# A decoder block with 32 routed experts: slots by row count, and expert weights addressed from registers

## The chip, the cores and the metric

The kernel runs on one core of a Trainium2 chip. The metric is device time in microseconds (us) of one execution, the median of the runs shown. Engines: PE (TensorE, matmul), DVE (VectorE), ACT (ScalarE), POOL (GpSimd), SP (SyncE, which here only issues DMAs); 16 DMA engines move data between the device's memory and the core.

## The reference

One layer of a decoder block: a token mixing half (two attention groups and an output projection) and a channel mixing half of routed experts. The change lies in the second half, which is

```python
def moe_ffn(h, w_router, b_router, w_mlp1, b_mlp1, w_mlp2, b_mlp2):   # 512 rows of 1024, 32 experts, top 4
    logits = xf @ w_router + b_router
    top_val, top_idx = lax.top_k(logits, TOP_K)
    gates = jax.nn.softmax(top_val, axis=-1)
    ...
    def expert_block(args):                          # the rows of one expert, e its number
        hid = xb @ w_mlp1[e] + b_mlp1[e]             # 1024 -> 2048
        glu = jnp.minimum(hid[..., ::2], SWIGLU_LIMIT)
        lin = jnp.clip(hid[..., 1::2], -SWIGLU_LIMIT, SWIGLU_LIMIT)
        act = glu * jax.nn.sigmoid(SWIGLU_ALPHA * glu) * (lin + 1.0)
        return act @ w_mlp2[e] + b_mlp2[e]           # 1024 -> 1024
    ...
    out = jax.ops.segment_sum(y * slot_gate, slot_tok)

x = x + gt2 * rms_norm(moe_ffn(h2, ...), g_post_ffn)
```

All tensors are float32. Each of the 512 rows goes to 4 of 32 experts, so an expert has 64 rows on average. The weights of one expert are 8 MB and 4 MB.

## The kernel before

**Order of the work.** The kernel is written as a list of operations. A planner (class `Plan`) orders them per engine: it simulates the engines with a cost for each operation, takes at each step the operation that can start first (ties by its place in the text plus a shift for its section), and gives out buffers as it goes. Each engine then runs its instructions strictly in that order, SP and POOL with their DMA issues too. All instructions are emitted from one place, so the profile shows nearly all of them on line 568. Tiles `u` are large buffers, `w` middle, `tiny` small ones, `bank` is a PSUM bank.

**Before the experts.** Attention and the output projection; then for each of four tiles of 128 rows: the norm (`wo_post`), router logits, top 4, gates and each row's place within its expert (`route`, lines 1426 to 1464). Places are in `posm16`, gates in `gate` and, split in three bfloat16 parts, in `aux`. `cnt` (1541) counts the rows of each expert, for a loop at the end (2065) that handles rows over 96 in extra blocks; its count is read into a register on every engine (2063). `b1` (1560) loads all biases into `b1r`, split in a high and a low part.

**One expert.** All 32 experts are handled alike, in the order of their number, with 96 slots each. `list_of` turns places into a list of row numbers for four experts at a time; `gather` (1619) fetches 96 rows of h2 by an indirect DMA on POOL, two experts ahead; `x_transposes` turns them. `bias_mm` starts three PSUM banks with the bias. `mm1` takes one load of weights (128 rows of `w_mlp1`, 1 MB) and multiplies; `swiglu`, `act_transposes`, then `mm2` with one load of `w_mlp2` (256 rows, 1 MB). An expert is 8 + 4 loads. `y_out` scales by the gate and `scatter` (1637) adds the 96 rows into an accumulator in the device's memory by an indirect DMA on POOL.

**Column tiles.** PE is used as four column tiles of 32 columns that work at the same time. With 96 slots there are three groups of 32 slots and four quarters of the output, 12 pieces, laid over three banks:

```python
def item(b, g):
    return (b, g) if g < 3 else (3, b)
```

**Weight loads.** `w_load` (1511) issues the loads on SP in a fixed sequence `seq` (1504): the first layer of expert e, then the second layer of expert e - 1. Up to ten loads (`DEPTH`) are ahead: load n waits for PE to have finished load n - 10 (1531). Addresses are constants.

**The end.** The last expert is not scattered. Its second layer comes in four loads of another shape; `split_last` splits each into a high and a low part on ACT, DVE and POOL, and `mm_last` multiplies the parts. `combine` (1810), in three column ranges, adds the last expert to the sums by a selecting matmul, adds the gated biases of the second layer, takes the norm and the residual and writes the output. `load_sums` (1801) reads the accumulator back, four tiles of 512 KB.

Of the kernel before, what the change touches and what calls it, by code (L numbers as in the profile page):

```python
# [26 lines left out]
E = 32  # L27
# [14 lines left out]
SLOTS = 96  # L42
EXTRA = 4
# [7 lines left out]
END_DVE = tuple((h, i) for h in (1, 2) for i in range(4))  # L51
SEL_RAW = (1, 2)
# [79 lines left out]
class Off:  # L132


    def __init__(self, view):
        self.view = view

# [137 lines left out]
class Plan:  # L275
# [107 lines left out]

    def after(self, o, *xs):
        for x in xs:
            o.deps[x.idx] = x
        return o
# [182 lines left out]
    @staticmethod  # L570
    def real(a):
        if isinstance(a, View):
            return a.real()
        if isinstance(a, Off):
            return bass.IndirectOffsetOnAxis(ap=a.view.real(), axis=0)
        return a


def build(tc, I, out, dbg=None):
# [752 lines left out]
    for t, b, g in ((gt1g, 0, 0), (gs2b, 1, 0), (sh2b, 0, 2)):  # L1332
# [22 lines left out]
                    op=ALU.add)  # L1355
    selb = const([P, 16, 12], F32, "selb")
    for b in range(3):
        V.tensor_copy(selb[:, :, 4 * b:4 * b + 3], selr[:, :, b:b + 1].to_broadcast([P, 16, 3]))
        V.tensor_copy(selb[:, :, 4 * b + 3:4 * b + 4], selr[:, :, 3:4])
# [6 lines left out]
    posm16 = const([P, NT, E], F16, "posm16")  # L1366
    cnt = const([P, E], F32, "cnt")
    aux = const([P, NT, E, 5], BF16, "aux")
# [57 lines left out]
    def route(i, r2):  # L1426
        with pl.sect(f"route{i}"):
# [31 lines left out]
            V.tensor_copy(aux[:, i, :, 2], gate[:, i, :])  # L1459
            g1 = small([P, E])  # L1460
            V.tensor_tensor(g1, gate[:, i, :], aux[:, i, :, 2], op=ALU.subtract)
            V.tensor_copy(aux[:, i, :, 3], g1)
            V.tensor_tensor(g1, g1, aux[:, i, :, 3], op=ALU.subtract)
            V.tensor_copy(aux[:, i, :, 4], g1)
# [45 lines left out]

    def w_load(n):
        e, s, j = seq[n]
        t = big((P, 2, D))
        if s and e == ne - 1:


            r, h = divmod(j, 2)
            src = w2_d[e * D + 512 * r:e * D + 512 * (r + 1), 512 * h:512 * (h + 1)].rearrange("(k p) n -> p k n", p=P)
            if j < 3:
                o = SP.dma_start(t.rearrange("p k (a n) -> p (k a) n", n=512), src)  # L1520
            else:
                for q in range(2):
                    o = SP.dma_start(t[:, q].rearrange("p (k n) -> p k n", n=256), src[:, :, 256 * q:256 * q + 256])
        elif s:

            o = SP.dma_start(t, w2_d[e * D + 256 * j:e * D + 256 * (j + 1), :].rearrange("(p k) n -> p k n", k=2))
        else:
            o = SP.dma_start(t.rearrange("p k n -> p (k n)"), w1[e * D + P * j:e * D + P * (j + 1), :])
# [11 lines left out]

    pl.gate = marks[6]
    with pl.sect("cnt"):

        pc = PS()
        with pl.group():
            for i in range(NT):
                T.matmul(pc[:, 0:E], lhsT=onesb, rhs=mkb[:, i, :], start=(i == 0), stop=(i == NT - 1))
        V.tensor_copy(cnt, pc[:, 0:E])
        NB = EXTRA * E
        fl = const([P, NB], F32, "fl")  # L1550
        for b in range(EXTRA):
            V.tensor_scalar(fl[:, b * E:(b + 1) * E], cnt, float(SLOTS + P * b), None, op0=ALU.is_gt)
        zero = small([P, NB])
        V.memset(zero, 0.0)
        incl = const([P, NB], F32, "incl")
        V.tensor_tensor_scan(incl, fl, zero, 0.0, ALU.add, ALU.add)
        nx_i = const([P, 1], I32, "nx_i")
        V.tensor_copy(nx_i, incl[:, NB - 1:NB])

    with pl.sect("b1"):  # L1560

        b1r = pl.buf((P, 2 * D), F32R, keep=True)
        for name, n in (("b_mlp1", 512), ("b_mlp2", 256)):
            b = w2((P, n))
            bH, bL = w2((P, n), F32R), w2((P, n), F32R)
            SP.dma_start(b, I[name].rearrange("l e (r n) -> (l e r) n", n=n))
            if n == 512:
                V.tensor_scalar(b[:, 1::2], b[:, 1::2], 1.0, None, op0=ALU.add)  # L1570
            A.copy(bH, b)
            V.tensor_tensor(bL, b, bH.bitcast(F32), op=ALU.subtract)
            for k, part_ in enumerate((bH, bL)):
                if n == 512:
                    for h in range(2):
                        SP.dma_start(b1r[64 * k:64 * k + 64, 512 * h:512 * h + 512].bitcast(F32),
                                     part_[64 * h:64 * h + 64, :].bitcast(F32))
                else:
                    SP.dma_start(b1r[64 + 32 * k:96 + 32 * k, D:2 * D].bitcast(F32), part_.bitcast(F32))

    pl.gate = None
# [4 lines left out]
    def one_hot(e, dt):  # L1586
        oh = w2((P, NT, SLOTS), dt)
        V.tensor_tensor(oh, slot16[:, 0:SLOTS].unsqueeze(1).to_broadcast([P, NT, SLOTS]),
                        posm16[:, :, e:e + 1].to_broadcast([P, NT, SLOTS]), op=ALU.is_equal)
        return oh  # L1590

    def list_of(es):
# [21 lines left out]
        for t in range(3):  # L1614
            V.tensor_copy(gg[96:128, 1 + t, :n], gg[32 * t:32 * t + 32, 0, :n])
        for a, e in enumerate(es):
            lists[e] = si[:, a:a + 1], gg[:, :, a:a + 1], gi[:, a:a + 1]
# [24 lines left out]
    def item(b, g):  # L1642
        return (b, g) if g < 3 else (3, b)
# [274 lines left out]
    def real(v):  # L1918
        return v.real()
# [171 lines left out]
```

## Time and profile before

| | |
|---|---|
| median of 3 runs | 1467.78 us (1466.84 to 1472.5) |
| the profiled execution's own time | 1467.23 us |
| its span, first to last instruction | 1465.5 us |
| mean granted clock of PE | 0.977 |
| busy: PE, DVE, ACT, POOL | 1405.5, 481.9, 283.3, 136.3 us |
| moved by DMA | 485.13 MB, 331 GB/s over the span |
| first weight step of the experts, and last scatter | 322.87 us, 1399.3 us |

How to read it: times are from one profiled execution. A group is a line, an engine, an operation and its tiles, with its count, its busy time, the mean of one in ns, and the idle time of the engine ahead of it with what ended that. PEld is the loading of PE's stationary side. DMA share is the mean busy share of the 16 engines. A busy PE includes modelled ends of pipelined matmuls.

### The profile page before, as it was taken

What the parts mean: (1) busy time and instruction counts of PE and PEld (TensorE: products, weight loads), DVE (VectorE), ACT (ScalarE), POOL (GpSimd) and SP (SyncE); (2) the same over time, 40 slices, a digit from 0 to 9 for tenths busy, and PEclk for the clock granted to TensorE, in tenths of its full rate; (3) what the DMA queues carried; (4) which work ended last, traced back from release to release, by engine and by line L of the source; (5) the groups of instructions that cost most, each with busy time, mean ns of one, the idle gap of its engine ahead of it and who ended that gap; (6) DMA issues with size and microseconds to landing.
All of it is one profiled execution on the core that took longest, in us unless ns stands there. A gap on an engine that the chain in (4) does not pass through costs nothing.

```text
span 1465.5 us, 33208 instructions
## 1 busy us (share of the span) xinstructions
PE 1405.5 (96%) x14622; PEld 681.9 (47%) x14622; DVE 481.9 (33%) x1310; ACT 283.3 (19%) x654; POOL 136.3 (9%) x182
## 2 busy tenths in 40 slices
PE   4999999989999999999999999999999999999985
PEld 2766568773444444444444444444444444434433
DVE  5689996771112211221211121122111211111134
ACT  4553596311010100010000000010100100011022
POOL 3000000400000000001000000000000001000023
PEclk8999999969999999999999999999999999999996
DMA  9928425349999999999999999999999999999951
GB/s 322 272 95 324 167 84 191 127 168 353 390 391 396 378 367 394 394 390 395 391 383 391 389 391 377 398 398 393 392 396 394 393 385 399 391 370 393 370 191 59
DMA packets 99297, 485.13 MB, mean 331 GB/s; under 512 B 14831, under 2 KB 33682, under 8 KB 48462
## 3 DMA queue, kind: packets, MB, share of 16 engines
q1 hardware_dynamic: 92206, 458.59, 80.6%
q0 software_dynamic: 6944, 24.38, 6.9%
q8 instruction: 116, 1.90, 0.5%
q14 instruction: 31, 0.25, 0.0%
HBM read 460.31 MB, written 20.07 MB: 328 GB/s over the span
## 4 chain that ended last, share of the span: by engine, by line
PE 88%; DVE 5%; DMA 3%; SPq 2%; issue 1%; ACT 1%; POOL 0%; DVEq 0%; POOLq 0%; ACTq 0%
PE bank L568 88%; DVE u L568 2%; SPq L568 2%; DVE w L568 2%; DMA u<-in_w_ada_dram 1%; DVE tiny L568 1%; DMA u<-qpart 1%; DMA u<-in_w_kv_b_dram 1%; ACT w L568 0%; DMA u<-h2d,tiny 0%; ACT u L568 0%; DVE aux L568 0%; DVE x L568 0%; DVE u L1967 0%; POOL tiny L568 0%
## 5 line engine op out<-in xcount | busy, mean ns | idle before, releaser
L568 PE MATMUL bank<-u,u 128*32 128x512 f32 (+2 forms) x12840 | 1176.8, 482 | 1.9 <-DVE w L568 0.9
L568 PEld LDWEIGHTS bank<-u,u 128*32 128x32 f32 (+1 forms) x12840 | 509.6, 115 | 600.5 <-issue 440.4
L568 DVE TENSOR_SCALAR u<-bank 128x256 f32<-128x256 f32 x96 | 38.7, 421 | 511.3 <-ACT u L568 281.1
L568 ACT ACTIVATE u<-bank 128x256 f32<-128x256 f32 x96 | 36.5, 383 | 550.0 <-PE bank L568 541.5
L568 DVE TENSOR_SCALAR u<-bank,tiny 96x256 f32<-96x256 f32 (+1 forms) x124 | 60.5, 488 | 239.0 <-PE bank L568 237.4
L568 POOL DMA_INDIRECT acc<-u,tiny x31 | 46.0, 1483 | 955.2 <-DVE w L568 663.6
L568 ACT COPY u<-bank 128x384 f32<-128x384 f32 (+3 forms) x115 | 50.0, 440 | 229.4 <-PE bank L568 207.3
L568 PE MATMUL bank<-ident,u 96*128 96x96 f32 (+1 forms) x472 | 66.5, 281 | 15.3 <-DVE u L568 13.6
L568 PEld LDWEIGHTS bank<-ident,u 96*128 96x128 f32 (+1 forms) x472 | 53.1, 172 | 57.6 <-issue 34.7
L568 DVE COPY u<-bank 128x64 f32<-128x64 f32 (+3 forms) x140 | 42.5, 342 | 111.6 <-PE bank L568 65.8
L568 PE MATMUL bank<-w,u 128*64 128x128 f32 (+4 forms) x472 | 55.8, 309 | 10.8 <-DMA u<-qpart 4.1
L568 ACT ACTIVATE u<-bank,tiny 96x512 f32<-96x512 f32 x31 | 21.2, 683 | 221.5 <-PE bank L568 221.5
L568 PEld LDWEIGHTS bank<-w,u 128*64 128x64 f32 (+1 forms) x472 | 45.7, 179 | 22.8 <-issue 11.8
L568 DVE TENSOR_TENSOR u<-u,u 128x1024 fp32r<-128x1024 f32 (+6 forms) x53 | 44.2, 853 | 6.7 <-ACT u L568 6.4
L568 DVE SCALAR_TENSOR_TENSOR u<-u,u 128x256 f32<-128x256 f32 (+1 forms) x99 | 43.5, 468 | 1.2
L568 ACT CAST u<-u 128x1024 fp32r<-128x1024 f32 (+4 forms) x48 | 36.2, 799 | 30.6 <-PE bank L568 20.7
L568 POOL DMA_INDIRECT u<-h2d,tiny x31 | 31.2, 1007 | 58.7 <-DVE tiny L568 20.3
L568 PE MATMUL bank<-u,w 128*128 128x512 f32 x104 | 34.9, 442 | 0.3 <-DVE w L568 0.2
L568 PE MATMUL bank<-u,condT 128*32 128x512 f32 x192 | 26.1, 639 | 8.5 <-DMA u<-in_w_ada_dram 7.2
L568 ACT COPY w<-bank 64x512 f32<-64x512 f32 (+5 forms) x67 | 29.9, 474 | 22.1 <-PE bank L568 18.0
L568 PE MATMUL bank<-ident,w 128*128 128x128 f32 (+2 forms) x192 | 29.6, 279 | 3.8 <-DVE w L568 2.0
L568 PE MATMUL bank<-w,w 128*128 128x512 f32 (+5 forms) x88 | 32.1, 468 | 0.9 <-DVE w L568 0.6
(155 smaller groups left out, 594.8 us busy)
## 6 DMA issues: line engine op xcount, KB each, us to landing
u<-in_w_mlp_dram SPq DMA_DIRECT2D x383, 1024.0 KB
u<-in_w_ada_dram SPq DMA_DIRECT2D x16, 1024.0 KB
u<-in_w_ada_dram SPq DMA_DIRECT2D x16, 512.0 KB
u<-in_w_o_dram SPq DMA_DIRECT2D x8, 512.0 KB
u<-in_w_in_dram SPq DMA_DIRECT2D x7, 512.0 KB
acc<-u SPq DMA_DIRECT2D x5, 512.0 KB
x<-in_x_dram SPq DMA_DIRECT2D x4, 512.0 KB
u<-in_w_in_dram SPq DMA_DIRECT2D x2, 1024.0 KB
```

The lines of the kernel that those rows point to most:

```text
L568: f(*[self.real(a) for a in args], **{k: self.real(a) for k, a in kw.items()})
```

## The change

**Positions.** The experts are handled in 32 positions instead of by number. Positions 0 to 3 hold experts 0 to 3, with 96 slots. The other 28 experts are sorted by their number of rows on the chip; the 16 largest go to positions of 96 slots, the 12 others to positions of 64 (`POS_RANK`: three of every eight positions, and the last two).

**Arranging.** A function `arrange`, called when expert 1 is set up, counts the rows, ranks the 28 experts by comparing all pairs (DVE on 28 x 28), writes the expert number of each position to `perm`, and permutes places, gates and counts (`posp16`, `gatep`, `cntp`). SP then reads the 28 expert numbers into registers, and the weight loads from position 4 on take their address from them. The biases of the first layer are gathered in position order by an indirect DMA; those of the first four come in directly, ahead.

**64 slots.** Two PSUM banks instead of three, `item` lays 2 x 4 pieces over them; gather, transposes, SwiGLU and scatter shrink alike. **The end:** the last expert has 64 slots and uses `mm2` like the others; `split_last` and `mm_last` are gone; `combine` works on two halves of 512 columns, with the bias matmuls of six of eight parts ahead of the last weights. **Extra blocks** use `perm` and the room of each position.

```diff
+FULL = 16
+POS_RANK = []
+_big, _small = list(range(FULL)), list(range(FULL, E - NS))
+for _n in range(E - NS):
+    POS_RANK.append((_small if _n >= E - NS - 2 or _n % 8 in (1, 4, 6) else _big).pop(0))
+ROOM = [96] * NS + [96 if _r < FULL else 64 for _r in POS_RANK]
...
+    def value(self, view, lo, hi):
+        v = Value(self.nc.sync, lo, hi)
+        c = ("SP", v, "value_load", (view,), {}, [], [view], (60.0, 0))
+        return v, self.add([c], None)
...
     def w_load(n):
         e, s, j = seq[n]
         t = big((P, 2, D))
-        if s and e == ne - 1:
...
+        def rows_of(src, r, m):
+            if e < NS:
+                return src[e * D + r:e * D + r + m, :]
+            return src[bass.ds(which[e][0].value * D + r, m), :]
+        if s:
+            o = SP.dma_start(t, Lazy(lambda: rows_of(w2_d, 256 * j, 256).rearrange("(p k) n -> p k n", k=2)))
         else:
-            o = SP.dma_start(t.rearrange("p k n -> p (k n)"), w1[e * D + P * j:e * D + P * (j + 1), :])
+            o = SP.dma_start(t.rearrange("p k n -> p (k n)"), Lazy(lambda: rows_of(w1, P * j, P)))
+        if e >= NS:
+            pl.after(o, which[e][1])
...
+    def arrange():
+        m = E - NS
...
+        with pl.sect("cnt"):
+            pc = PS()
+            with pl.group():
+                for i in range(NT):
+                    T.matmul(pc[:, 0:E], lhsT=onesb, rhs=mkb[:, i, :], start=(i == 0), stop=(i == NT - 1))
+            V.tensor_copy(cnt, pc[:, 0:E])
+            key, rank = small([P, m]), small([P, m])
+            V.scalar_tensor_tensor(key, cnt[:, es], float(E), tie[:, es], op0=ALU.mult, op1=ALU.add)
+            rows_by_cols(along(key), across(key), ALU.is_gt, rank)
+            put = rows_by_cols(along(rank), across(rpos[:, es]), ALU.is_equal)
+            V.tensor_copy(perm[:, 0:NS], ecol[:, 0:NS])
+            rows_by_cols(put, along(ecol[:, es]), ALU.mult, perm[:, es])
+            perm_i = const([1, E], I32, "perm_i")
+            V.tensor_copy(perm_i, perm[0:1, :])
+            for p in range(NS, ne):
+                which[p] = pl.value(perm_i[0:1, p:p + 1], NS, E - 1)
             for i in range(NT):
+                places = small([P, m])
+                rows_by_cols(put, along(posm16[:, i, es]), ALU.mult, places)
+                V.tensor_copy(posp16[:, i, es], places)
+                rows_by_cols(put, along(gate[:, i, es]), ALU.mult, gatep[:, i, es])
+                gate_parts(i, es)
+        with pl.sect("b1"):
...
+            G.indirect_dma_start(out=b, out_offset=None, in_=b1_d, in_offset=Off(frm), bounds_check=P - 1, oob_is_err=True)
...
+            halves_of(b, 512, lambda k: [(64 * k, 512 * h, slice(64 * h, 64 * h + 64)) for h in range(2)])
...
     def gather(e):
-        xg = big((SLOTS, D))
+        xg = big((ROOM[e], D))
...
-    def item(b, g):
+    def item(m, b, g):
+        if m == 64:
+            return 2 * b + g // 2, g % 2
         return (b, g) if g < 3 else (3, b)
...
-            for b in range(3):
+            for b in range(len(hid)):
                 for g in range(4):
-                    n, t = item(b, g)
+                    n, t = item(m, b, g)
...
+            if e == 1:
+                arrange()
...
-        act = act_transposes(fa, True)
-        y = [PS()[0:SLOTS, 0:n] for n in (512, 256, 256)]
+        act = act_transposes(fa)
+        y = [PS()]
+        open_ = {(i, h): bias_of(i, h) for i in range(3) for h in range(2)}
         for j in range(4):
-            w = split_last()
-            r = j // 2
-            mm_last(y[1:] if j % 2 else y[:1], lambda c: (act[:, 4 * r + c, :], act[:, 8 + 4 * r + c, :]), w, j < 2, j == 3)
-            for h in {2: (0,), 3: (1, 2)}.get(j, ()):
-                combine(h)
+            mm2(y, act, j)
+        combine(y[0], open_)
```

The five steps of `route` that split the gates of 32 experts become `gate_parts` on four columns, with two copies of four columns ahead (places and gates of experts 0 to 3); the constants that `arrange` needs are filled on GpSimd with 44 small instructions ahead of the experts.

More of the change, by code (lines that the diff above doesn't have):

```diff
@@ L136, in __init__, with value_load @@
         self.view = view
+class Lazy:
+    def __init__(self, make):
+        self.make = make
+class Value:
+    def __init__(self, engine, lo, hi):
+        self.engine, self.lo, self.hi, self.value = engine, lo, hi, None
+    def value_load(self, ap):
+        self.value = self.engine.value_load(ap, min_val=self.lo, max_val=self.hi)
 class Buf:
@@ L1458, in route, with gate_parts @@
             V.tensor_scalar(gate[:, i, :], ex, sg, None, op0=ALU.mult)
[L1459 to L1464, printed above, removed]
+            for to, frm in ((posp16, posm16), (gatep, gate)):
+                V.tensor_copy(to[:, i, 0:NS], frm[:, i, 0:NS])
+            gate_parts(i, slice(0, NS))
+    def gate_parts(i, es):
+        a = aux[:, i, es]
+        g1 = small([P, es.stop - es.start])
+        V.tensor_copy(a[:, :, 2], gatep[:, i, es])
+        V.tensor_tensor(g1, gatep[:, i, es], a[:, :, 2], op=ALU.subtract)
+        V.tensor_copy(a[:, :, 3], g1)
+        V.tensor_tensor(g1, g1, a[:, :, 3], op=ALU.subtract)
+        V.tensor_copy(a[:, :, 4], g1)
     first = []
@@ L1509, in build @@
     raws = {}
+    which = {}
     def w_load(n):
@@ L1539, in w_next, with halves_of @@
         return raws.pop(n)
-    pl.gate = marks[6]
-    with pl.sect("cnt"):
-        pc = PS()
-        with pl.group():
-            for i in range(NT):
[L1547 to L1550, printed above, removed]
+    b1r = pl.buf((P, 2 * D), F32R, keep=True)
+    def halves_of(b, n, put):
+        m = b.shape[0]
+        bH, bL = w2((m, n), F32R), w2((m, n), F32R)
+        A.copy(bH, b)
+        V.tensor_tensor(bL, b, bH.bitcast(F32), op=ALU.subtract)
+        for k, part_ in enumerate((bH, bL)):
+            for r, c, frm in put(k):
+                SP.dma_start(b1r[r:r + frm.stop - frm.start, c:c + n].bitcast(F32), part_[frm, :].bitcast(F32))
@@ L1667, in mm2 @@
         w = w_next()
+        m = act.shape[2]
         for k in range(2):
-            with pl.group(3 * 429.0):
-                for b in range(3):
+            with pl.group(m / 32 * 429.0):
+                if m == 64:
                     for g in range(4):
-                        n, t = item(b, g)
-                        c0 = 256 * (b % 2)
-                        T.matmul(y[b // 2][32 * g:32 * g + 32, c0:c0 + 256], lhsT=act[:, 2 * j + k, 32 * t:32 * t + 32],
-                                 rhs=w[:, k, 256 * n:256 * n + 256], start=(j + k == 0 and b % 2 == 0),
-                                 stop=(j == 3 and k == 1), skip_group_check=True)
@@ L1677, in mm2 @@
[L1677 to L1702 removed]
+                        n, t = item(m, 0, g)
@@ L1823, in combine @@
+        def combine(y, open_):
+            gt2g, sel, ss, _, _ = fin
+            g2 = lists[ne - 1][3]
+            ysH, ysL = w2((P, 512), F32R), w2((P, 512), F32R)
+            A.activation(ysH, y, AF.Copy, scale=g2)
+            V.scalar_tensor_tensor(ysL, y, g2, ysH.bitcast(F32), op0=ALU.mult, op1=ALU.subtract)
             for i in range(NT):
                 sl = slice(i * P, (i + 1) * P)
[L1825 to L1829 removed]
@@ L1919, in real @@
         return v.real()
-    incl, fl, slot16, pcol, posm16, gate, aux, nx_i, pow_e, ident, b1r, gt2g = [
-        real(v) for v in (incl, fl, slot16, pcol, posm16, gate, aux, nx_i, pow_e, ident, b1r, fin[0])]
+    incl, fl, slot16, pcol, posp16, gatep, aux, nx_i, pow_e, ident, b1r, gt2g, perm, room = [
+        real(v) for v in (incl, fl, slot16, pcol, posp16, gatep, aux, nx_i, pow_e, ident, b1r, fin[0], perm, room)]
     x1, fas, h2s = [[real(v) for v in vs] for vs in (x1, fas, h2s)]
```

342 lines of the change are left out of this document (191 added, 151 removed).

## The prediction, made before the result was known

> **What bounds the kernel now.** I read the page first (busy time by engine, the slices, the idle time ahead of the matmul group), then a table by stretches of time for the expert stage, then the DMA queues of that stage, the issues on SyncE's queue, the time line of one expert, and last the end.
>
> ```profile
> span 1465.5 us, 33208 instructions
> PE 1405.5 (96%) x14622; PEld 681.9 (47%) x14622; DVE 481.9 (33%) x1310; ACT 283.3 (19%) x654; POOL 136.3 (9%) x182
> L568 PE MATMUL bank<-u,u 128*32 128x512 f32 (+2 forms) x12840 | 1176.8, 482 | 1.9 <-DVE w L568 0.9
> ```
>
> PE is busy 96% of the span, and ahead of the 12,840 expert matmuls it sat idle for 1.9 us in all, none of it for a DMA. That reads as bound by PE. The next view, busy time by stretch with the DMA share and rate in the last two columns, says that this is half of it.
>
> ```profile
> 430.00:1340.00 910.00, 910.00 (x10739) 380.30 (x10735) 171.15 (x491) 84.61 (x191) 64.20 (x53) 1.00 1.01 390
> 405.00:410.00 5.00, 5.00 (x100) 2.99 (x92) 1.52 (x5) 0.38 (x1) 0.00 (x0) 1.00 1.02 424
> 415.00:420.00 5.00, 5.00 (x46) 2.35 (x38) 3.26 (x9) 1.38 (x3) 1.45 (x1) 1.00 1.02 419
> 420.00:425.00 5.00, 5.00 (x52) 1.81 (x52) 0.00 (x0) 0.48 (x1) 0.99 (x1) 1.00 1.02 332
> 425.00:430.00 5.00, 5.00 (x52) 1.49 (x48) 0.00 (x0) 0.00 (x0) 0.00 (x0) 1.00 1.04 307
> 440.00:445.00 5.00, 5.00 (x97) 2.99 (x93) 0.21 (x1) 0.00 (x0) 0.00 (x0) 1.00 1.02 421
> ```
>
> Over 910 us of experts the 16 DMA engines are as full as PE (share 1.01). With weights alone in the queues they move 419 to 424 GB/s; where an expert's gather and scatter pass (420 to 430) it is 332 and 307. The queues of the same stretch:
>
> ```profile
> q1 hardware_dynamic: 45801, 333.51, 91.5%
> q0 software_dynamic: 5714, 20.06, 9.1%
> u<-in_w_mlp_dram SPq DMA_DIRECT2D x318, 1024.0 KB
> ```
>
> 318 loads in 910 us are 2.86 us a load, so 34.3 us an expert (12 loads). At 421 GB/s a load of 1,048,576 B takes 2.49 us, so 12 take 29.9; the other 4.4 us go to gather, scatter and instruction fetch. And PE:
>
> ```profile
> 706.21 0.13 PEld L568 LDWEIGHTS bank<-u,u 128*32 128x32 f32 x4 [0.30 <-issue]
> 710.50 0.13 PEld L568 LDWEIGHTS bank<-u,u 128*32 128x32 f32 x4 [0.30 <-issue]
> 728.03 0.88 PE L568 MATMUL bank<-ident,u 96*128 96x96 f32 x8
> ```
>
> Ten groups of four column tiles take 4.29 us, 0.429 us a group. A load feeds three banks of four tiles, each in two passes, so six groups, 2.57 us, and 12 loads 30.9 us; transposes (one set 0.88), bias and lists make up the rest of 34.3. So 96 slots put PE and the DMA engines at the same 34.3 us by coincidence. Which of them is a little ahead shows at the end of the stream:
>
> ```profile
> L568 SPq DMA_DIRECT2D u<-in_w_mlp_dram x385: 327/328/1111, 139.6 to 1396.9; - x193
> 1401.00:1404.00 3.00, 3.00 (x30) 0.95 (x26) 0.00 (x0) 0.00 (x0) 0.00 (x0) 1.00 1.11 357
> 1404.00:1407.00 3.00, 3.00 (x36) 0.91 (x32) 0.00 (x0) 1.02 (x1) 0.00 (x0) 1.00 0.53 111
> 1407.00:1410.00 3.00, 3.00 (x36) 0.91 (x32) 0.00 (x0) 0.02 (x1) 0.00 (x0) 1.00 0.03 8
> ```
>
> The last load is issued at 1396.9 and the engines run dry at 1407: some 10 us, four loads, lie queued in front of the engines. A queue that is never empty means that taking work off PE brings no weight in sooner. The DMA stream is what I keep, and its end at 1407 is the pivot of the sum.
>
> **The change, part by part.**
>
> *PE work of twelve experts.* A 64-slot expert needs two banks instead of three: four groups a load, 1.72 us, so 12 x 0.86 = 10.3 us less an expert, 124 us in all. Of this I count nothing in the stream, because the DMA engines cover it (2.49 us a load). What it does bring is the end: PE, today four queued and six landed loads behind, will have used each weight soon after it lands.
>
> *Gather and scatter of 64 rows.* A third of the rows goes in twelve experts. By queue 0's share a pair costs 0.091 x 910 / 26.5 = 3.1 us, by the stretch above up to 4.4; a third is 1.04 to 1.47, and I take 1.25, as neither row is nearer: 12 x 1.25 = 15 us off the stream. If the cost is per transfer rather than per row, it is 0.
>
> *28 register loads on SyncE's queue.* The expert numbers are read by SyncE one by one, all ready together, so they stand behind each other, and the weight loads queue behind them. The nearest row is the one register load that the kernel has today:
>
> ```profile
> L2063 SPq TENSOR_LOAD <-nx_i x1: 528/528/528, 1456.2 to 1456.2; - x1
> ```
>
> 28 x 0.53 = 15 us, with a move each (an estimate) up to 20. The four queued loads cover 10 us of it; afterwards the engines idle. Bounds: 0 (if loads are put in between) and 20 (no queue in front at that moment). I take 8, since the row gives 15 and the refill of the pipe 2 or 3 more, less the 10. Later loads need address arithmetic, which has a whole 2.86 us for an issue of 0.33; cover gone, it would cost 336 times the excess.
>
> *Arranging on DVE.* Some 22 operations on 28 x 28 elements and 35 small ones, gated on expert 0's first step.
>
> ```profile
> L568 DVE TENSOR_TENSOR u<-x,u 128x512 f32<-128x512 f32 x4 | 2.7, 688 | 0.0
> 336.01 0.85 PE L568 MATMUL bank<-ident,u 96*128 96x96 f32 x8 [1.69 <-DMA u<-h2d,tiny]
> ```
>
> Scaled from 688 ns for 512 elements, 784 take about 1 us: 22 + 7 = 29 us, hidden by a DVE that is busy 171 of 910 us there. But queued behind those are the small steps of the first row lists, for which the first gather waits, and at 336 PE waited 1.69 us for that gather. Bounds 0 and 5; I take 1, because all of expert 0 is still PE's cover. The counting and bias steps that move out of the stage before, and the five gate steps per tile that shrink from 32 columns to four there, lie beside other waits: 0. The 44 small fills on GpSimd fall in a stage where it is idle: 0. The bias now also comes by an indirect gather of 128 rows of 2 KB and SBUF copies, 0.26 + 0.5 MB, while the engines are full: 2 us at 421 GB/s, bounds 0 and 4.
>
> *The end.* Today:
>
> ```profile
> 1415.26 5.40 DVE L568 SCALAR_TENSOR_TENSOR u<-u,u 128x256 f32<-128x256 f32 x3
> 1421.96 12.89 PE L568 MATMUL bank<-u,u 128*96 128x512 f32 x72 [0.57 <-ACT u L568]
> 1432.06 0.69 ACT L568 ACTIVATE w<-bank,tiny 96x512 fp32r<-96x512 f32 x1 [6.75 <-PE bank L568]
> 1432.78 0.75 DVE L568 SCALAR_TENSOR_TENSOR w<-bank,tiny,w 96x512 fp32r<-96x512 f32 x1 [8.11 <-ACT w L568]
> 1437.22 0.68 DVE L568 TENSOR_TENSOR u<-bank,u 128x512 f32<-128x512 f32 x1
> 1448.89 1.27 DVE L568 SCALAR_TENSOR_TENSOR u<-u,tiny,x 128x1024 f32<-128x1024 f32 x1
> 1450.19 5.92 SPq L568 DMA_DIRECT2D out_dram<-u  x4
> 1452.14 3.60 POOL L568 TENSOR_TENSOR u<-u,x 128x512 f32<-128x512 f32 x2
> ```
>
> 58.5 us pass between the last weight (1407) and the end (1465.5): PE finishes its first product, SwiGLU waits in line with the splitting of weights on DVE, then 12.9 us of split matmuls, then the combination. After the change the last four loads arrive at 2.49 us each and need 1.72, the splitting is gone, and the row sums, 2 MB queued behind the last weights, arrive one by one in 5 us. After the last weight: 1.7 (last step) + 0.7 + 0.75 + about 1.8 for the selecting matmuls and hand-overs = 5 to the first addition; then DVE has four tiles of 2 x 0.68 + 0.69 + 0.3 + 1.27 = 3.6, so 14.4; 1.8 for GpSimd's last addition; and 9.4 from the last output issue (1456.1) to the end. That is 31 us, bounds 28 (DVE work of tiles spread) and 36 (PE not quite caught up).
>
> **Sum.** 1407 - 15 + 8 + 1 + 2 = 1403 for the last weight, + 31 = 1434 for the span. The profiled execution took 1467.2 us for its span of 1465.5, so 1.7 lie around it: 1436, against 1467.2 and a median of 1467.8.
>
> Two rules are weighed here. The page "DMA: Bandwidth & Descriptors" of the Trainium skill (Where 436 GB/s comes from) says that HBM to SBUF is held to about 358 GB/s for a core, with 435 as the ceiling of the fabric. The stretches at 419 to 424 disagree with the first and come close to the second: by 435 a load would take 2.41 us and the stream could be 30 us shorter at the very best. It speaks against hoping for the 124 us of PE time.
>
> **The rivals.** (1) PE decides and the engines have room: for it stands the 1.9 us of idle time, against it the share of 1.01 and the 10 us queue. The time would be 1467 - 124 - 15 = 1328.
> (2) The other side: a weight load whose address stands in a register is served more slowly by the DMA engines (shorter pieces, or a gap at each). Place: 336 loads of experts 4 to 31. From 2.49 + 31/336 = 2.58 us a load on the gain is gone; at 2.7 it costs 336 x 0.21 = 70, so 1506. Against it: the last loads of today come in other, shorter pieces and still run at 391 to 401.
>
> ```profile
> 1395.00:1398.00 3.00, 3.00 (x48) 1.29 (x44) 1.44 (x3) 0.68 (x1) 0.00 (x0) 1.00 1.05 401
> 1398.00:1401.00 3.00, 3.00 (x26) 0.84 (x22) 0.51 (x2) 0.00 (x0) 1.41 (x1) 1.00 1.05 391
> ```
>
> (3) PE starves between loads and falls to half its clock:
>
> ```profile
> 1416.00:1419.00 3.00, 0.88 (x4) 0.25 (x2) 3.00 (x2) 1.32 (x2) 3.00 (x2) 0.89 0.00 0
> 1422.00:1425.00 3.00, 3.00 (x7) 1.89 (x8) 2.44 (x6) 3.00 (x7) 0.56 (x1) 0.50 0.88 336
> 1425.00:1428.00 3.00, 3.00 (x21) 2.58 (x20) 0.00 (x0) 0.31 (x1) 3.00 (x2) 0.98 0.87 307
> ```
>
> After an idle stretch of 6 us the granted clock is 0.50, and back at 0.98 three us later. Held at half, a 64-slot expert would need 2 x 24 = 48 us against the stream's 33: 12 x 15 = 180 more, 1616; it decides from a mean clock under 24/33 = 0.73. Against it: a slow PE has no gaps, so the clock returns, as in the third row, and the ten buffers bridge it. The page "TensorE: Matmul & The Clock Gate" (What's actually happening) of the Trainium skill puts the window at 3.4 us; these rows agree with a window of that order, and my gaps of 0.8 us a load are under it.
> (4) No change: rows save nothing, register loads cost all 20 and the end needs 40: 1407 + 20 + 3 + 40 = 1470.
> (5) It doesn't do what it says: 64 slots overflow and the loop of extra blocks runs, each at least 12 loads, 30 us: 1466 or more. Routing the reference's inputs gives 12 of the 28 experts over 64 rows, and the 17th largest has 62, so no block is left over.
>
> **How the numbers follow.** The forecast gets 0.83, (1) 0.03, (2) 0.05, (3) 0.01, (4) 0.07, (5) 0.01. The forecast's own bounds: 1407 - 17.6 + 28 + 1.7 = 1419 with every unknown at its good end; 1407 - 12.5 + 20 + 5 + 4 + 36 + 1.7 = 1461 with every one at its bad end (and rows at queue 0's share). I take 1417, for small holes of today's stream that may close, to 1460, just short of all bad together. About 0.5%, 7 us, can be told from no change. Faster by more: the forecast nearly whole and (1), 0.84; same 0.09; slower 0.07.
>
> **What would show it.** Right: PE idle for DMA in the 64-slot experts while the DMA share stays at 1.0 and the rate between gathers at about 421 GB/s; PE busy down by some 120 us with the span down by 31; some 30 us from the engines running dry to the end; one hole of 5 to 10 us in the DMA share during experts 0 to 2, beside 28 register loads in a row. Wrong: a DMA share well under 1 with PE full (1); weight-only stretches under 410 GB/s (2); a clock under 1.00 between 430 and 1340 (3); no hole, or one of 20 us, for the register step; scatter stretches as long as before for the row step.

## The result, and the profile after

The changed kernel took 1433.28 us (median of 4 runs, 1430.29 to 1435.53) against 1469.28 us before (4 runs, 1466.84 to 1472.5): ratio 0.9752, 95% interval 0.9723 to 0.9782. The forecast was 1436. The profiled execution took 1434.52 us for a span of 1432.8. A second measurement (E5 below) gave 1433.23 us and 0.9769 (0.9746 to 0.9792).

The page of the profile after, span, busy times and the expert matmuls (columns as before; the program's lines have moved, L568 is L600 now):

```profile
span 1432.8 us, 29541 instructions
PE 1291.5 (90%) x12386; PEld 584.6 (41%) x12386; DVE 478.8 (33%) x1315; ACT 264.5 (18%) x622; POOL 131.4 (9%) x223
L600 PE MATMUL bank<-u,u 128*32 128x512 f32 (+3 forms) x10648 | 1071.6, 507 | 79.1 <-DMA u<-in_w_mlp_dram 74.8
```

PE lost 114 us of busy time and the span lost 32.7; ahead of the expert matmuls PE now sits idle for 79.1 us (1.9 before), 74.8 of them until a weight load. That is the picture of a transfer-bound stage. Busy time by stretches of the changed kernel: the whole expert stage, a 64-slot expert between two gathers, and the stretch around the register loads.

```profile
430.00:1340.00 910.00, 842.11 (x9106) 318.00 (x9102) 156.20 (x452) 76.83 (x182) 65.93 (x54) 0.99 1.02 398
505.00:510.00 5.00, 3.85 (x32) 0.83 (x32) 0.42 (x1) 0.43 (x2) 0.00 (x0) 1.00 1.02 423
355.00:360.00 5.00, 5.00 (x52) 1.43 (x44) 4.97 (x14) 0.00 (x0) 0.00 (x0) 1.00 0.75 264
360.00:365.00 5.00, 5.00 (x52) 1.56 (x48) 4.74 (x10) 0.00 (x0) 0.00 (x0) 1.00 0.38 159
365.00:370.00 5.00, 5.00 (x52) 1.55 (x48) 3.77 (x11) 0.69 (x2) 0.00 (x0) 1.00 0.00 0
370.00:375.00 5.00, 5.00 (x96) 2.87 (x90) 4.44 (x9) 0.47 (x2) 0.00 (x0) 1.00 0.01 3
```

The DMA share stayed at 1.02 over 910 us with PE at 842; the weight-only stretch runs at 423 GB/s although its addresses stand in registers. From 360 to 375 the engines were dry for 5 x 0.62 + 5 x 1.00 + 5 x 0.99 = 13 us, beside these instructions on SyncE's queue (duration in ns min/median/max, first and last start):

```profile
L162 SPq TENSOR_LOAD <-perm_i x28: 262/262/492, 358.1 to 373.6; - x28
L162 SPq FUSED_REGOPS  x28: 147/147/192, 358.6 to 373.9; - x28
L162 SPq SEQ_ASSERT  x28: 18/18/29, 358.8 to 374.1; - x28
```

A register load costs 0.26 us here, not 0.53, but each brings two instructions that check its bounds. The three together are 0.43 us, and the triples follow each other every 0.57 us, so some 0.15 us of each shows as no instruction; 28 of them take 16 us, from 358.1 to 374.1. PE did not stop (5.00 of 5 us busy): it lived on loads that had landed.

The DMA queues from 430 to 1340 (packets, MB, share of the 16 engines; of the issues the size and the median us to landing):

```profile
q1 hardware_dynamic: 47019, 342.36, 92.9%
q0 software_dynamic: 5267, 18.14, 8.2%
u<-in_w_mlp_dram SPq DMA_DIRECT2D x325, 1024.0 KB, 22.0
```

Seven more loads than before in the same 910 us, 2.80 us a load instead of 2.86. Two things changed in these rows. Queue 0 (gather and scatter) fell from 9.1 to 8.2%, which is 8 us. And the weights became cheaper: 0.929 x 910 / 342.36 = 2.469 us of engine time per MB, against 0.915 x 910 / 333.51 = 2.497 before. The second was not in the prediction.

The end, first by time line (start, duration, engine), then by stretches of 3 us:

```profile
1388.55 2.95 PE L600 MATMUL bank<-u,u 128*32 128x512 f32 x18 [0.56 <-DMA u<-in_w_mlp_dram]
1391.98 0.75 PE L600 MATMUL bank<-ident,u 128*128 128x128 f32 x4 [0.48 <-DVE u L600]
1392.77 1.75 SPq L600 DMA_DIRECT2D u<-acc  x4
1394.04 8.77 PE L600 MATMUL bank<-u,u 128*32 128x512 f32 x64 [1.30 <-DVE u L600]
1402.88 0.69 ACT L600 ACTIVATE w<-bank,tiny 128x512 fp32r<-128x512 f32 x1 [9.22 <-PE bank L600]
1404.93 1.29 DVE L600 TENSOR_TENSOR u<-bank,u 128x512 f32<-128x512 f32 x2 [0.58 <-PE bank L600]
1412.99 9.87 SPq L600 DMA_DIRECT2D out_dram<-u  x4
```

```profile
1386.00:1389.00 3.00, 2.37 (x20) 0.57 (x24) 0.00 (x0) 0.00 (x0) 0.56 (x1) 1.00 0.70 295
1389.00:1392.00 3.00, 2.41 (x19) 0.67 (x11) 1.44 (x4) 0.77 (x2) 0.00 (x0) 1.00 0.52 221
1392.00:1395.00 3.00, 1.70 (x12) 0.83 (x16) 0.76 (x3) 0.53 (x2) 0.00 (x0) 0.97 0.69 262
1395.00:1398.00 3.00, 3.00 (x20) 0.87 (x16) 0.00 (x0) 0.00 (x0) 0.00 (x0) 0.50 1.02 407
1398.00:1401.00 3.00, 3.00 (x32) 0.87 (x28) 0.00 (x0) 0.00 (x0) 0.00 (x0) 0.96 0.70 272
1401.00:1404.00 3.00, 2.19 (x21) 0.48 (x13) 0.40 (x1) 0.69 (x1) 0.00 (x0) 1.00 0.15 61
```

All 64 matmuls of the last expert's second layer stand in one run, after SwiGLU and its transposes: PE did not wait for weights, the weights waited for SwiGLU. The run took 8.77 us; in the third to fifth stretch the granted clock is 0.97, 0.50 and 0.96, so some 3 us of it ran at half clock. When the last weights were in can be read from the packets' sizes: weights come in packets of 8 KB (a row of `w_mlp1`, two of `w_mlp2`), the row sums, asked for from 1392.77 on, in packets of 4 KB. The packets that start from 1397 to 1397.7, then from 1397.7 to 1398:

```profile
DMA packets 75, 0.32 MB, mean 451 GB/s; under 512 B 5, under 2 KB 5, under 8 KB 70
DMA packets 29, 0.11 MB, mean 355 GB/s; under 512 B 3, under 2 KB 3, under 8 KB 29
```

Of the five larger ones in the first row one belongs to the instruction queue, four are weights; after 1397.7 none starts. So the last weights were in at 1398, and PE, which ended its run at 1394.04 + 8.77 = 1402.8, was 4.8 us behind them.

### The profile page after: what moved, and what is told of

Its sections match the earlier page's. It is cut to its first block, busy times and chain, and to the rows that moved or that the text cites. A ratio compares the mean times of both kernels' runs of the same rounds, so it can differ in the third digit from the quotient of the medians.

```text
span 1432.8 us, 29541 instructions
## 1 busy us (share of the span) xinstructions
PE 1291.5 (90%) x12386; PEld 584.6 (41%) x12386; DVE 478.8 (33%) x1315; ACT 264.5 (18%) x622; POOL 131.4 (9%) x223
## 4 chain that ended last, share of the span: by engine, by line
## 5 line engine op out<-in xcount | busy, mean ns | idle before, releaser
L600 PE MATMUL bank<-u,u 128*32 128x512 f32 (+3 forms) x10648 | 1071.6, 507 | 79.1 <-DMA u<-in_w_mlp_dram 74.8
L600 PEld LDWEIGHTS bank<-u,u 128*32 128x32 f32 (+1 forms) x10648 | 420.8, 115 | 667.8 <-issue 357.3
L600 DVE TENSOR_SCALAR u<-bank 128x256 f32<-128x256 f32 x84 | 34.3, 422 | 529.4 <-ACT u L600 290.4
L600 ACT ACTIVATE u<-bank 128x256 f32<-128x256 f32 x84 | 32.1, 383 | 564.0 <-PE bank L600 561.3
L600 POOL DMA_INDIRECT acc<-u,tiny x31 | 45.4, 1464 | 909.6 <-DVE w L600 350.1
L600 DVE TENSOR_SCALAR u<-bank,tiny 32x256 f32<-32x256 f32 (+2 forms) x91 | 47.3, 520 | 208.4 <-PE bank L600 129.6
L600 ACT COPY u<-bank 128x384 f32<-128x384 f32 (+4 forms) x117 | 45.3, 402 | 231.9 <-PE bank L600 218.6
L600 DVE COPY u<-bank 128x64 f32<-128x64 f32 (+5 forms) x131 | 42.9, 351 | 100.2 <-ACT u L600 58.0
L600 PEld LDWEIGHTS bank<-ident,u 128*128 128x128 f32 (+2 forms) x448 | 49.4, 172 | 51.6 <-issue 32.8
L600 PE MATMUL bank<-ident,u 128*128 128x128 f32 (+2 forms) x448 | 61.7, 278 | 8.3 <-DVE u L600 8.3
L600 PE MATMUL bank<-w,u 128*64 128x128 f32 (+4 forms) x472 | 54.5, 304 | 8.2 <-DVE w L600 3.6
L600 ACT ACTIVATE u<-bank,tiny 96x512 f32<-96x512 f32 (+1 forms) x31 | 21.2, 683 | 209.8 <-PE bank L600 209.8
L600 PEld LDWEIGHTS bank<-w,u 128*64 128x64 f32 (+1 forms) x472 | 44.1, 174 | 20.3 <-issue 7.7
L600 DVE TENSOR_TENSOR u<-u,u 128x1024 fp32r<-128x1024 f32 (+6 forms) x47 | 41.1, 897 | 3.0 <-ACT u L600 2.8
L600 PE MATMUL bank<-u,condT 128*32 128x512 f32 x192 | 27.6, 678 | 8.7 <-DMA u<-in_w_ada_dram 6.3
L600 ACT COPY w<-bank 64x512 f32<-64x512 f32 (+5 forms) x67 | 29.9, 474 | 25.9 <-PE bank L600 21.8
L600 POOL DMA_INDIRECT u<-h2d,tiny x31 | 31.5, 1015 | 30.3 <-DVE tiny L600 21.5
L600 PE MATMUL bank<-u,w 128*128 128x512 f32 (+1 forms) x92 | 33.3, 462 | 0.3 <-DVE w L600 0.3
L600 DVE SCALAR_TENSOR_TENSOR u<-u,u 128x256 f32<-128x256 f32 (+1 forms) x85 | 33.3, 423 | 0.6
L600 PE MATMUL bank<-ident,w 128*128 128x128 f32 (+2 forms) x192 | 30.0, 282 | 4.0 <-DMA w<-in_b_ada_dram 2.0
L600 ACT CAST u<-u 128x1024 fp32r<-128x1024 f32 (+4 forms) x40 | 28.4, 747 | 20.0 <-PE bank L600 10.5
L600 PE MATMUL bank<-w,w 128*128 128x512 f32 (+4 forms) x80 | 26.2, 453 | 2.0 <-ACT w L600 1.0
## 6 DMA issues: line engine op xcount, KB each, us to landing
u<-in_w_mlp_dram SPq DMA_DIRECT2D x384, 1024.0 KB, 21.8
```

The costliest lines, as they stand in the source:

```text
L600: f(*[self.real(a) for a in args], **{k: self.real(a) for k, a in kw.items()})
```

## The experiments

All ratios are against the kernel before on the same chip; 0.005 of it is 7 us. For the changed kernel the mean of its two measurements, 0.9760, is used.

**E1: the register loads apart.** The 28 reads move from one place to 28, each ahead of the first load of its expert.

```diff
-    which = {}
+    which, numbers = {}, []
...
     def w_load(n):
         e, s, j = seq[n]
+        if e >= NS and e not in which:
+            which[e] = pl.value(numbers[0][0:1, e:e + 1], NS, E - 1)
+            pl.after(which[e][1], tails[n - DEPTH - 1])
...
-            for p in range(NS, ne):
-                which[p] = pl.value(perm_i[0:1, p:p + 1], NS, E - 1)
+            numbers.append(perm_i)
```

> The changed kernel, with the 28 register loads no longer in a row: each expert number is read on SyncE's queue just ahead of that expert's first weight load. Everything else stays. Theory (the DMA engines' stream sets the end): the dry stretch beside the register loads (362 to 375, 13 us) goes, since one load of 0.56 us now stands between weight loads that are 2.5 us apart; the last weight lands 13 us earlier and the time is 1433 - 13 = 1420 (1416 to 1425), 0.966 of before. Rival (the hole is covered further on, because buffers and PE then set the pace): 1430 to 1436. Rival (a register load in the middle of the stream holds up the queue each time): 1433 or more, with small holes in the DMA share at each expert.

1421.96 us (1420.46 to 1424.14), ratio 0.9699 (0.9673 to 0.9725): 11.3 us under the changed kernel by medians, 0.0061 x 1467 = 9 by ratios, give or take 5. The register loads and the same stretches in this version:

```profile
L162 SPq TENSOR_LOAD <-perm_i x28: 263/268/491, 420.9 to 1313.7; - x28
```

```profile
360.00:365.00 5.00, 5.00 (x52) 1.48 (x48) 4.26 (x13) 0.38 (x1) 0.00 (x0) 1.00 0.98 334
365.00:370.00 5.00, 5.00 (x88) 2.73 (x84) 3.71 (x6) 0.77 (x2) 0.00 (x0) 1.00 1.00 395
370.00:375.00 5.00, 5.00 (x97) 2.99 (x93) 5.00 (x16) 0.00 (x0) 0.00 (x0) 1.00 1.01 423
```

The same 28 loads, and no hole (shares 0.98, 1.00, 1.01). So the loads' standing in a row was the price, and it reached the end nearly whole. At the end of this trace (packets that start from 1382 to 1382.5, then the run of 64):

```profile
DMA packets 52, 0.22 MB, mean 442 GB/s; under 512 B 5, under 2 KB 5, under 8 KB 47
1378.71 10.03 PE L600 MATMUL bank<-u,u 128*32 128x512 f32 x64 [1.30 <-DVE u L600]
```

From 1382.5 on every packet is smaller than 8 KB, so the last weights were in at 1383, 15 us ahead of the changed kernel's (11 ahead of its second trace, E5, where they were in at 1394).

**E2: 96 rows moved, 64 computed.** In the twelve 64-slot experts only the transfers go back.

```diff
...
-        xg = big((ROOM[e], D))
+        xg = big((SLOTS, D))
...
-        return xg
+        return xg[0:ROOM[e]]
...
-            ys = big((m, D))
+            ys = big((SLOTS, D))
...
-                A.activation(ys[:, 0:512], y[0][0:64, :], AF.Copy, scale=g2[0:64])
...
+                A.activation(ys[:, 0:512], y[0][0:96, :], AF.Copy, scale=g2[0:96])
...
+                A.activation(ys[64:96, 512:1024], y[0][64:96, :], AF.Copy, scale=g2[64:96])
```

> The changed kernel, but the twelve 64-slot experts gather and scatter 96 rows again (the last 32 of them are unused; they go to the spare rows of the sums), while their matmuls stay at 64 slots. One small operation of ScalarE per expert is added. Theory as predicted (each row costs DMA time, 1.25 us per expert for 32 + 32 rows): 1433 + 11 x 1.25 to 1433 + 12 x 1.25 = 1447 to 1448 (the last expert has no scatter in either). Rival (cost per transfer, not per row): 1433 to 1436. Rival (the rows were worth all of the 26 us that the stream regained behind the register loads): 1457 to 1460.

The 26 us of the expectation are meant as what the stream made up: it ended 9 us earlier than before (1407 against 1398; 13 earlier in E5's trace) in spite of a hole of 13 us. That is 22 to 26 us; the trace before holds no landing times of single loads by which it could be told better.

1447.47 us (1444.61 to 1452.1), ratio 0.9872 (0.9846 to 0.9897): 14.2 us more by medians, 16 by ratios. The queues of the stage:

```profile
q1 hardware_dynamic: 46621, 339.47, 92.1%
q0 software_dynamic: 5731, 20.08, 9.0%
```

Queue 0 is back at its old 9.0%, and the time is up by what the prediction had put on the rows (15). The cost is per row, and the rows are not the whole of the 22 to 26. In the 910 us alone less of it shows: queue 0 has 7 us more, and 2.9 MB of weights fewer, 7 us at 2.469, came in; where the rest of the 14 to 16 lies was not found. But the weights stay at 0.921 x 910 / 339.47 = 2.469 us per MB, so their getting cheaper isn't the rows' doing.

**E3: 26 positions of 96 slots.** Rows and PE's work come back in ten experts.

```diff
-FULL = 16
+FULL = 26
...
-    POS_RANK.append((_small if _n >= E - NS - 2 or _n % 8 in (1, 4, 6) else _big).pop(0))
+    POS_RANK.append((_small if _n >= E - NS - 2 else _big).pop(0))
```

> The changed kernel with 96 slots for the 26 largest of the sorted experts instead of 16; only the last two positions keep 64 slots. So PE's work comes back in ten experts (10 x 10.3 = 103 us), their rows too, and the sorting, the register loads and the short end stay. Theory (the DMA stream sets the end, PE's work is under it): 1433 + 10 x 1.25 = 1446, up to 1452 if PE, again level with the stream, has less time to catch up in the last two experts. The same as the kernel with 96 rows moved and 64 computed, within 5 us. Rival (PE's work counts): 1433 + 26 = 1459 or more, up to 1433 + 103 = 1536 if it counts in full.

1447.88 us (1446.0 to 1451.35), ratio 0.9873 (0.9849 to 0.9898): the same as E2, so that 103 us of PE work seem to cost nothing (2 to 3 us, if the rows of two experts that E2 moves and E3 doesn't are counted). The expert matmuls and the weights' issues:

```profile
L600 PE MATMUL bank<-u,u 128*32 128x512 f32 (+3 forms) x12568 | 1152.7, 485 | 8.7 <-DMA u<-in_w_mlp_dram 6.3
```

```profile
q1 hardware_dynamic: 46370, 337.63, 92.0%
u<-in_w_mlp_dram SPq DMA_DIRECT2D x318, 1024.0 KB, 20.0
```

It was the theory's number, but the test was weaker than I took it to be: this version still has the hole of the register loads. I take it that the hole holds the stream back so far that PE, even with its work back, stays close behind it: a load is issued 20.0 us before it lands, so buffers come free long before their loads arrive. E10 asks again without the hole.

**E4: constant addresses.** The reference's order is written into the program.

```diff
-            return src[bass.ds(which[e][0].value * D + r, m), :]
+            return src[ORDERED[e] * D + r:ORDERED[e] * D + r + m, :]
```

> The changed kernel, but the weight addresses are constants: the sorted order for the reference's inputs is written into the program, and the reading of the 28 numbers and the address arithmetic on SyncE are left out (the rest of the arranging is still computed). Theory (only the 13 us hole was the price of the registers): the same as with the register loads spread out, 1420 (1416 to 1425), within 3 us of it. Rival (a load with its address in a register is dearer each time): faster than the spread version by 336 times the excess, 10 us or more. Rival (the hole is not worth its length): 1430 to 1436.

1424.26 us (1422.61 to 1426.77), ratio 0.9711 (0.9687 to 0.9735), the same as E1 within the interval. 336 loads addressed from registers and 28 spread reads cost nothing that can be measured.

**E5: the changed kernel once more.** No edit.

> The changed kernel itself once more, so that it stands beside the variants on one chip. By every theory 0.975 of before (0.972 to 0.978), as in its first measurement; the spread version measured 0.970.

1433.23 us (1429.44 to 1435.51), ratio 0.9769 (0.9746 to 0.9792).

**E6: twelve positions of 96 slots, register loads apart.** E1 with `FULL = 12` and 64 slots also at every other position up to the 26th.

> The version with spread register loads, and 96 slots for only the 12 largest of the sorted experts instead of 16 (16 positions of 64, no expert over its room on these inputs). Theory (rows count, PE's work doesn't): four experts' gather and scatter lose a third, 4 x 1.06 to 4 x 1.25 = 4 to 5 us, so 1422 - 4.5 = 1417, ratio 0.967 (0.964 to 0.970). Rival (PE's work counts): 4 x 10.3 = 41 us, 1381. Rival (per transfer): 1422.

1420.03 us (1411.73 to 1423.75), ratio 0.9677 (0.9649 to 0.9705). The direction fits the rows (4 to 5 us), the size can't be told from nothing; what is excluded is that PE's work counts in full, 41 us.

**E7: the last expert's first layer earlier.** E6 with one constant changed.

```diff
-EARLY_L = 2
+EARLY_L = 6
```

> As the version with 12 positions of 96 slots and spread register loads, but of the last expert's eight first-layer loads six, not two, come ahead of the second-layer loads of the expert before it. Theory for the end (PE's last 64 matmuls stand in one run behind SwiGLU, and run partly at half clock, so PE ends 5 to 6 us after the last landing and not the 1.7 that the prediction had): SwiGLU is done before the last weights land, PE ends 2 to 3 us after the last landing, and the time is 2 to 4 us under the version before, 1414. Rival (the scatter of the expert before the last now comes later, and the row sums wait for it): 0 to 5 us more, 1417 to 1422.

1418.83 us (1416.41 to 1419.47), ratio 0.9669 (0.9648 to 0.969): no difference from E6 that can be measured. The run of 64 in E6, then in E7:

```profile
1375.49 7.07 PE L600 MATMUL bank<-u,u 128*32 128x512 f32 x64 [1.30 <-DVE u L600]
```

```profile
1374.54 7.30 PE L600 MATMUL bank<-u,u 128*32 128x512 f32 x64 [1.30 <-DVE u L600]
```

In both it still waits for the transposes of SwiGLU's output, and E7's starts 0.95 us earlier only. In both traces no packet of 8 KB starts after 1379.2, so the last weights were in at 1379.5 and PE ended 3.1 us (E6) and 2.3 us (E7) behind them. The 2 to 3 us of the expectation were thus there nearly without the change; what failed is that moving four loads would free PE of SwiGLU. In E6 the run has the full clock by its stretches,

```profile
1375.50:1379.00 3.50, 3.50 (x36) 1.11 (x40) 0.00 (x0) 0.00 (x0) 0.00 (x0) 1.00 0.97 390
1379.00:1382.60 3.60, 3.56 (x36) 0.86 (x28) 0.00 (x0) 0.00 (x0) 0.00 (x0) 1.00 0.71 282
```

so half clock cost the changed kernel 8.77 - 7.07 = 1.7 us, and E1 10.03 - 7.07 = 3.0.

**E8: weights unsorted.** E4 with `ORDERED = list(range(32))`.

> The version with constant addresses, but with the weights read in the order 0 to 31 as before the change, while the rows stay in sorted order: rows meet other experts' weights, so only times are read. Question: the weights' packets took a little less engine time per MB after the change (2.47 us per MB in 430 to 1340) than before it (2.50), also with all rows and nearly all of PE's work put back (2.48). Theory (the order in which the experts' weights are read makes it): about 2.50 here, some 7 us on the span. Rival (it is the depth of the queue or PE's lighter load): 2.47 as with the sorted order, and the same span within 3 us of 1421.

A single run of 1426.3 us, span 1424.6; the queue of the stage:

```profile
q1 hardware_dynamic: 46972, 342.02, 92.8%
```

0.928 x 910 / 342.02 = 2.469 us per MB, as in the sorted order. That theory falls.

**E9 and E11: fewer loads ahead.** E1 with `DEPTH = 8` and `DEPTH = 6` instead of 10.

> The version with spread register loads, with at most 8 instead of 10 weight loads ahead of PE, so that fewer loads lie queued in front of the DMA engines. Question: why the weights' packets take 2.47 us of engine time per MB after the change and took 2.50 before it. Theory (a longer queue is served a little faster): 2.48 to 2.50 here, small dry spots in the stream as before the change, 1422 + 4 to 10 = 1426 to 1432. Rival (depth beyond what keeps the engines fed counts nothing): 2.47 and 1422, within 3 us. Third way (eight are too few to bridge the waits at expert borders): well over 1432.

> The version with spread register loads, with at most 6 weight loads ahead of PE. With 8, the wait from issue to landing stayed at 12 to 15 us in most of the stream, so the queue in front of the DMA engines had hardly become shorter; with 6 it should be about 8 to 10 us, as before the change and in the version with spare matmuls (5 to 11). PE stays at its light load. Theory (a short queue in front of the engines makes the weights' packets dearer and leaves small dry spots): 2.49 to 2.50 us per MB and over 4 us of dry spots in 430 to 1340. Rival (PE's reading makes the packets dearer): 2.47 as with 10 and 8 loads, whatever the dry spots do. The time is expected over that with 8 (1430), 1435 to 1460 by either.

1430.33 us (1429.4 to 1433.32), ratio 0.9764 (0.9748 to 0.9779) with 8; 1443.37 us (1439.73 to 1450.01), ratio 0.9851 (0.9812 to 0.989) with 6. Queues and issues of the version with 8, then with 6, and of E1, which has 10:

```profile
q1 hardware_dynamic: 46841, 341.11, 92.6%
u<-in_w_mlp_dram SPq DMA_DIRECT2D x323, 1024.0 KB, 17.9
```

```profile
q1 hardware_dynamic: 46320, 337.28, 92.0%
u<-in_w_mlp_dram SPq DMA_DIRECT2D x322, 1024.0 KB, 13.0
```

```profile
q1 hardware_dynamic: 47147, 343.32, 93.0%
u<-in_w_mlp_dram SPq DMA_DIRECT2D x328, 1024.0 KB, 21.8
```

With the wait from issue to landing going 21.8, 17.9, 13.0 us, the cost per MB goes 2.465, 2.470, 2.482. The step to 2.470 says nothing, as versions with ten loads ahead lie between 2.465 and 2.469; the step to 2.482 is clear, but smaller than the 2.49 that the theory wanted. Nor is it the greater part of the price. Over 384 loads of 1.049 MB 0.017 us per MB make 7 us, while E11 is 22 us over E1. The shares of queues 0, 1 and 8 together fall from 101.6% (E1) to 101.1% (E9) and 100.6% (E11), which is 5 and 9 us of the 910 in dry spots.

**E10: PE's old work without the rows.** E1 with spare matmuls in ten of the 64-slot experts.

```diff
...
+            for g in range(4 if "h" in spare else 0):
+                T.matmul(spare["h"][32 * g:32 * g + 32, :], lhsT=x[:, k, 0:32], rhs=w[:, 512 * g:512 * g + 512],
+                         start=(k == 0), stop=(k == 7), skip_group_check=True)
...
+                    for g in range(4 if "y" in spare else 0):
+                        T.matmul(spare["y"][32 * g:32 * g + 32, 0:256], lhsT=act[:, 2 * j + k, 0:32],
+                                 rhs=w[:, k, 256 * g:256 * g + 256], start=(j + k == 0), stop=(j == 3 and k == 1),
+                                 skip_group_check=True)
```

> The version with spread register loads, with PE given its old work back in ten of the twelve 64-slot experts by spare matmuls: a third group of four column tiles of each product goes into a spare bank whose contents nobody reads. Rows moved stay at 64, so this is PE's work alone, 10 x 10.3 = 103 us. Theory (PE's work is under the DMA stream): 1422 (1420 to 1426); the weights' packets may go from 2.465 to 2.48 us per MB as in the version with 26 positions of 96 slots, worth 3 to 4 us. Rival (PE's slack is worth the whole of what the stream regained beyond the rows, some 10 us): 1430 to 1434. Rival (PE's work counts in full): 1422 + 103.

1432.48 us (1427.53 to 1435.45), ratio 0.977 (0.9748 to 0.9792): 10.5 us over E1 by medians and by ratios, give or take 5. The theory's 1422 to 1426 is missed, the rival's 10 us is met. Matmuls, then queue and issues:

```profile
L600 PE MATMUL bank<-u,u 128*32 128x512 f32 (+2 forms) x11928 | 1150.1, 502 | 3.3 <-DVE u L600 2.3
```

```profile
q1 hardware_dynamic: 46325, 337.34, 92.7%
u<-in_w_mlp_dram SPq DMA_DIRECT2D x320, 1024.0 KB, 10.6
```

PE waits for no weight any more (no load in its line), a load is issued only 10.6 us before it lands, and its MB costs 0.927 x 910 / 337.34 = 2.501 us: the picture of the kernel before. The expert stage, and the packets from 1394 to 1394.7:

```profile
430.00:1340.00 910.00, 910.00 (x10234) 360.06 (x10226) 154.86 (x452) 77.86 (x182) 65.48 (x54) 1.00 1.01 391
DMA packets 11, 0.06 MB, mean 82 GB/s; under 512 B 4, under 2 KB 4, under 8 KB 4
```

PE is busy for all of the 910 us, and the last weights (the seven packets of 8 KB in the second row, after which none starts) are in at 1395, 12 us after E1's. About 103 us of PE work (counted at 0.429 us a group; the busy time of PE rose by 78 us, from 1288.6 to 1366.9; the rest may have filled gaps inside what E1 shows as busy) are worth some 10 us, not 0 and not 103.

Who paces whom here can be estimated. Ten loads ahead at 910 / 320 = 2.84 us make 28 us from a load's issue to PE's last use of it. With 10.6 us to landing and 2.6 of use, a load lies landed for some 15 us before PE turns to it. In E1 the same sum is 10 x 910 / 328 = 27.7, less 21.8 and 1.7 to 2.6: some 4 us. So with its old work PE paces the stream, though the DMA engines look full too (1.01); without it the stream paces PE.

## Why the prediction was right, and where not

1436 against 1433.3. The main step was right: in the changed kernel the stream of weights sets the end, not PE's busy time. Shown by PE's 114 us bringing 36, by 75 us of PE idle until a weight load at a DMA share of 1.02, and by E10 and E6, where most of PE's work proves to be worth nothing. For the kernel before it was not quite right: there, by the picture of E10, PE was the bound, by some 10 us in 1467, with the stream close behind. And the sum came out so near by luck: errors of both signs met in it. Part by part:

- **Rows, -15 forecast:** -14 to -16 by E2. Right, and per row as argued.
- **PE's work, 0 in the stream forecast:** -10 by E10. This is the step that failed: "A queue that is never empty means that taking work off PE brings no weight in sooner." The queue was not empty, but PE paced it: a load was issued only when PE let a buffer go, and loads lay landed ahead of PE (the "six landed loads" of the prediction say the same, and ahead of the 12,096 matmuls in column tiles, the experts' own among the 12,840, PE never sat idle). The stream alone could go a little faster. With PE's work back the packets cost 2.501 us per MB, without it 2.465; over 384 loads of 1.049 MB that is 384 x 1.049 x 0.036 = 14.5 us (an estimate from the 910 us), beside 12 us between the last weights of the two traces and the 10.5 measured. Whether the dearer packets are the cause of the 10 us, or only what the engines show when PE paces them, no run tells apart. Nor is it known what makes them dearer: E11 has 2.482 at 13.0 us from issue to landing with a light PE, E3 2.480 at 20.0 with a full one, so either seems to do something.
- **Register loads, +8 forecast:** +9 to +11 by E1, a hole of 13 us. The 16 us that they take were met by luck: 28 x 0.53 = 15 came from a load of twice the length, and the checks weren't in it. The cover was wrong: I counted on the 10 us of queue that the end of the trace before showed, but 16 us of loads made a hole of 13, so there were 3 us. From 350 to 355, ahead of the first register load, the share was only 0.72 already.
- **The two don't simply add.** With the hole there, PE's work is worth 2 to 3 us (E3 against E2); without it, 10 (E10 against E1). And the hole costs 9 to 11 us beside a light PE, but only 2 to 3 beside a full one (E3 less the rows of ten experts, 12.5 us by the forecast, against E10). That is as it should be where the later of two paths sets the end, PE's or the stream's; with intervals of 5 us on each difference it is a reading, not a proof.
- **Arranging and bias, +3 forecast:** no run priced them. E1's stretches show DVE at 3.7 to 5.0 of 5 us beside a full stream, which may be what hides it.
- **The end, 58.5 to 31 us forecast:** 58.5 to 35, counted from the last weights (1398) to 1432.8. "After the change the last four loads arrive at 2.49 us each and need 1.72" failed: the last steps stood behind SwiGLU. PE ended at 1402.8, 4.8 us after the last weights and not 1.7; of the 3.1 between, 1.7 are the half clock. The rest held: from there 30.0 us against 31 - 1.7 = 29.3.

Together, by the traces: the stream ended 9 us earlier (1407 to 1398) where 4 were forecast, and the end is 24 us shorter where 27.5 were. Both misses are 4 to 5 us, and they cancel. The stream's 9 are the sum of larger steps: 1407 before, 1395 in E10 (rows gone, PE's work there, no hole), 1383 in E1, 1398 with the hole.

Of the rivals, "PE decides" (1328) falls by E6 and E10, in which 41 us of PE work taken away and 103 added moved the time by 2 and 10.5 us. "Loads addressed from registers are served more slowly" falls by the 423 GB/s and by E4. "No change" needed rows that save nothing and register loads at 20; E2 and E1 have 15 and 10. The clock between 430 and 1340 was 0.99; a clock under 1.00 was named as the sign of rival (3), but 0.99 is far from the 0.73 at which it would have decided. Where it did cost was at the very end, a place that I hadn't looked at.

By the rows of the end, the clock was at half for 0.06 x 3 + 3 + 0.08 x 3 = 3.4 us. The page "TensorE: Matmul & The Clock Gate" of the Trainium skill (What's actually happening) says that the clock is decided in windows of about 3.4 us that run freely; this stretch agrees. So do two others. In E5 the stretch about the start of the run of 64,

```profile
1388.00:1391.00 3.00, 1.70 (x12) 0.75 (x15) 0.58 (x2) 0.53 (x2) 0.00 (x0) 0.77 0.73 265
1391.00:1394.00 3.00, 3.00 (x20) 0.64 (x16) 0.00 (x0) 0.00 (x0) 0.00 (x0) 0.66 1.03 415
```

has 0.46 x 3 + 0.68 x 3 = 3.4 us at half (a mean of 0.77 is half clock for 0.46 of the stretch), and E1, with 0.65, 0.50 and 0.71 in three such stretches from 1377 to 1386, has 6.8, twice as much. What sets it off is open: up to about the start of the run PE was busy for 6.5 of 9 us in the changed kernel (1386 to 1395), and for 6.5 of 9 in E6 as well (1366 to 1375), where the clock stayed at 1.00.

## What to carry to other kernels

When two resources look level, ask which one waits: if loads lie landed ahead of the consumer, the consumer paces, however full the transfers look. Taking work off it then helps until the transfers take over, here by 10 us of 103; measure that by adding the work back alone (E10), and don't put it at zero. A row of scalar loads on the queue that issues the transfers was here a hole nearly as long as the row: read the cover at that very moment, and put the loads one by one in front of their first use (E1, 9 to 11 us). And at the end of a stream ask what paces the last consumer: here the activation between two layers, not the last load, and a clock that fell to half, 3 us together. Spread register loads with fewer 96-slot positions (E6, E7) beat both kernels, at 0.968 and 0.967 of the time before.

## What the hardware showed that was not expected

- The time that a weight's packets need isn't fixed: 2.465 to 2.501 us per MB over 910 us, in the same kind of stream. It goes with the length of the queue and with PE's load; the cause is only narrowed down.
- A register load on SyncE takes 0.262 us in a row and 0.268 alone (E1), the first of each 0.49, where the only one of the kernel before took 0.528. With two checking instructions of 0.147 and 0.018 us one number takes 0.57 us in a row.
- From 12 to 6 us before the last weights were in, the DMA share fell to about a half (0.70 and 0.52 from 1386 to 1392, at 295 and 221 GB/s), though every weight had been asked for by 1378. I read it as some engines having finished their part of the last loads while others were behind. In E10, with its shorter queue, the share was still 1.02 from 1386 to 1392 (411 and 431 GB/s), 3 us before its last weights. Nothing here tested why.
